# A reordered prologue, filled scan ends and six early output blocks in a hybrid decoder kernel

## Chip, cores and metric

The kernel runs on one core of a Trainium2 chip. The metric is the device time of one execution in microseconds (us). The engines are called PE (matrix products; PEld is its weight load), DVE (vector), ACT (scalar functions), POOL (general) and SP (which here only issues DMA transfers). An fp32 product is two PE instructions, one with the suffix "fp32r" types is one.

## What is computed

The program is a two-layer decoder trunk over T = 272 tokens (16 learned ones and 256 given) of width 2048. The change touches the first layer's mixing part only; what it has to compute, cut from the reference:

```python
h = rms_norm(h0, mix_norm_g)
xx = token_shift(h) - h
xr, xw, xk, xv, xa, xg = (h + xx * mu[i] for i in range(6))
r, k, v = xr @ w_r, xk @ w_k, xv @ w_v
w = -softplus(-(dec_w0 + tanh(xw @ dec_w1) @ dec_w2)) - 0.5
decay = exp(-exp(w))
a = sigmoid(a_w0 + (xa @ a_w1) @ a_w2)
g = sigmoid(xg @ g_w1) @ g_w2
kk = k * k_k, per head of 64 divided by its norm
k = k * (1 + (a - 1) * k_a)
for t in tokens, per head:
    state = state * d_t - (state @ kk_t) (kk_t a_t)^T + v_t k_t^T
    y_t = state @ r_t
out = ((group_norm(y) + bonus) * g) @ w_o
h1 = h0 + out
```

A SwiGLU, a stick-breaking attention and a second SwiGLU follow, from about 730 us on, and are the same in both kernels.

## The kernel before

Everything is kept transposed, channels on partitions and the 272 tokens along the free axis. A 2048x2048 matrix is 16 blocks of 128 output channels; a block is 16 steps k of 128 input channels. In most places a weight w and an activation x are each split in a high and a low part (`whi`, `wlo`, `hi`, `lo`: ACT casts, DVE subtracts), and `mm3k` (L186 to L188) makes one step of three products, whi·hi, whi·lo and wlo·hi; a block then has 48 products of 272 columns.

**Prologue** (L412, `prologue`). `load_tokens` (L313) issues 16 loads of 128x272, in turns on SP's and ACT's queue, with the small vectors on ACT's. ACT squares each (L424), DVE adds four at a time (L428), and PE sums over channels with four fp32 products (L429). ACT takes Ln and Exp (L434, L435), DVE one Newton step. Then the blocks of the key projection w_k: the first G0 = 3 are made with unsplit fp32 weights and activations (L481), k by k in step with the shifted, mixed input x; the other 13 use split weights. `key_out` copies a key block, squares it and adds its squares with an fp32 product into a sum per head, and after the 8th and the 16th block the key norms follow (maximum, Ln, Exp, Newton) and are stored to a scratch in DRAM. Beside them a generator (`rest`) makes the mixed inputs and the three narrow projections (`lr`, dec_w1, a_w1, g_w1; L551), whose weights come in four sets through the pool `wx` (L545), which the split key weights use too.

**Scan** (L617, `scan`). 16 pairs of heads, four chunks of 64 tokens each. Turn n works on four pairs: A = n is finished (states, y, group norm, gate), M = n+1 has its triangular inverse made, B = n+2 is scored, C = n+3 gets decay, iclr and gate from the narrow projections. M's inverse goes through POOL (16x16 blocks, by way of DRAM) and is then widened on PE: `left` (yb) and `right` (zb) for blocks of 16 and 32; yb is followed by a copy on DVE, Ys, which zb reads. A's norm is `parts` (sums per head on PE), an Ln and an Exp on ACT and the last products on DVE. PE and SP take the instructions in the order in which the program writes them; the other engines' order is set by the scheduler at build time.

Between these steps `fill(k)` pulls k steps of three products from `stream`: v and r of all pairs, then 60 steps of the output projection w_o for 4 blocks (15 of their 16 steps; the last needs the last pair). A usual turn takes 32 steps. In the last three turns the number is 0.625 of that. After the scan `wo_first` ends the four blocks, makes the other twelve and adds h0.

The lines that matter: L424 to L442 squares and rstd, L465 to L485 weights and the fp32 blocks, L488 `key_out`, L536 to L553 the narrow projections, L391 to L396 two constants `blk`, L637 to L700 the turns, L772 `stream`, L820 `wo_first`.

Of the kernel before, what the change touches and what calls it, by code (L numbers as in the profile page):

```python
# [25 lines left out]
HD = 64  # L26
# [14 lines left out]
G0 = 3  # L41
# [5 lines left out]
DRAIN = 0.625  # L47
PSTEP = 8
NHEAD = 4
KHEAD = 13  # L50
# [6 lines left out]
def _consts():  # L57
# [14 lines left out]
    put("cen", np.eye(128) - blk / 64)  # L72
    pi = p[:, None] % 64
# [26 lines left out]
    put("blk", blk)  # L100
# [18 lines left out]
class Builder:  # L119
# [99 lines left out]
    def proj(self, src, acts, nk=NK, m=128, late=False):  # L219
        w = self.weights(src, nk, m)  # L220
        out = (self.scbank("mm") if late else self.mmbank())[:m, :acts[0][-1].shape[1]]
# [136 lines left out]
    def time_mix(self):  # L358
# [9 lines left out]
            tc.tile_pool(name="dr", bufs=2, space=bass.MemoryType.DRAM))  # L368
        self.prologue(hid)
        self.o = []  # L370
        self.oraw = []
        with ExitStack() as ctx:
            sp = ctx.enter_context(tc.tile_pool(name="sp", bufs=1, reuse_waits="tile"))
            self.l2 = ctx.enter_context(tc.tile_pool(name="l2", bufs=2, reuse_waits="tile"))
# [32 lines left out]
    def prologue(self, hid):  # L407
# [3 lines left out]
        with ExitStack() as ctx:  # L411
# [33 lines left out]
            def xtile():  # L445
                return pt.tile([128, T], F32, name="xi", tag="xi", bufs=NXL)
# [43 lines left out]
            def key_out(m, ps):  # L490
# [10 lines left out]
                if m % 8 < 7:  # L501
                    return
# [928 lines left out]
```

## Time and profile before

| | us |
|---|---|
| median of 3 runs | 2698.18 |
| lowest and highest of them | 2696.77, 2700.59 |
| the profiled execution | 2704.42 |
| its span | 2702.6 |
| start of the first key product | 28.35 |
| start of the scan's first product (zw) | 174.98 |
| end of the scan's last product wait (L186) | 656.43 |

Rows of a timeline give the start of an instruction or of a run of like ones, its length, engine, line, operation, output<-input, shapes, the number of instructions in the run, and in brackets how long its engine had been idle just before and which instruction it waited for. Rows of the stage table give a window, its length, the busy time of PE, PEld, DVE, ACT and POOL with their instructions, the granted clock of PE (1.00 is 2.4 GHz), the share of the DMA engines and the GB/s moved.

### The profile page before, as it was taken

The numbers are of one execution on the slowest core, as the hardware profiler recorded it, in microseconds if no ns is written. First come the engines' busy times: TensorE is split into PE (matmuls) and PEld (weight loads), VectorE is DVE, ScalarE is ACT, GpSimd is POOL, SyncE is SP. The second block draws the span as 40 slices with busy tenths as digits, with TensorE's granted clock in tenths as the row PEclk, the third lists the DMA queues.
The fourth block names the chain that finished last, engine by engine and source line by source line (L and its number), as shares of the span: only waits on it lengthen the run. The fifth ranks groups of instructions, "written<-read, shape, count | busy, mean of one in ns | idle before, by whom it ended". The sixth has DMA issues, their size and how long they took to land.

```text
span 2702.6 us, 53996 instructions
## 1 busy us (share of the span) xinstructions
PE 2647.7 (98%) x20942; PEld 2452.3 (91%) x20942; DVE 1788.1 (66%) x3610; ACT 1493.0 (55%) x3012; POOL 166.5 (6%) x477
## 2 busy tenths in 40 slices
PE   6999999999999999999999999999999999999999
PEld 5888888888999999999999999988888888888888
DVE  6676767676665555555566875688766666666665
ACT  5675666665544444444445764577555455554553
POOL 0004342431000000000000000000000000000000
PEclk9999999999999999999999999999999999999999
DMA  5434333435555555555655555433665665665655
GB/s 185 140 112 124 101 118 94 125 84 164 172 179 163 188 174 165 187 175 164 187 177 162 183 170 173 158 123 109 194 189 180 195 190 177 201 188 177 198 178 180
DMA packets 185908, 439.50 MB, mean 163 GB/s; under 512 B 58515, under 2 KB 89779, under 8 KB 185651
## 3 DMA queue, kind: packets, MB, share of 16 engines
q1 hardware_dynamic: 183632, 433.23, 51.6%
q8 instruction: 164, 2.69, 0.4%
q10 hardware_dynamic: 2016, 2.82, 0.3%
q14 instruction: 96, 0.76, 0.1%
HBM read 430.24 MB, written 5.74 MB: 161 GB/s over the span
## 4 chain that ended last, share of the span: by engine, by line
PE 92%; DVE 3%; DMA 2%; issue 2%; ACT 2%; POOL 0%; SPq 0%; ACTq 0%; DVEq 0%; POOLq 0%
PE mm L192 22%; PE mm L186 16%; PE mm L188 16%; PE mm L187 16%; PE mm L191 12%; DMA raw<-w_k 1%; PE lr L551 1%; PE mm L481 1%; PE cb L1343 1%; DVE wlo L216 1%; PE cb L1335 1%; PE wa L1292 1%; PE z L972 1%; PE zb L1281 1%; PE yb L1262 1%
## 5 line engine op out<-in xcount | busy, mean ns | idle before, releaser
L168 DVE TENSOR_TENSOR wlo<-raw,whi 128x512 fp32r<-128x512 f32 (+1 forms) x1444 | 977.2, 679 | 613.7 <-ACT whi L167 593.4
L167 ACT CAST whi<-raw 128x512 fp32r<-128x512 f32 (+1 forms) x1444 | 877.6, 610 | 859.6 <-PE mm L187 536.3
L186 PE MATMUL mm<-hl,whi 128*128 128x272 f32 x3344 | 971.1, 291 | 1.5 <-ACT hl L258 1.5
L188 PE MATMUL mm<-hl,wlo 128*128 128x272 f32 x3344 | 966.6, 289 | 0.0
L187 PE MATMUL mm<-hl,whi 128*128 128x272 f32 x3344 | 964.9, 289 | 0.0
L192 PE MATMUL mm<-hl,whi 128*128 128x512 f32 x2624 | 919.8, 394 | 0.0
L191 PE MATMUL mm<-hl,wlo 128*128 128x256 f32 x2624 | 738.2, 282 | 0.0
L186 PEld LDWEIGHTS mm<-hl,whi 128*128 128x128 f32 x3344 | 630.1, 188 | 12.0 <-issue 9.5
L187 PEld LDWEIGHTS mm<-hl,whi 128*128 128x128 f32 x3344 | 636.3, 190 | 0.5 <-issue 0.4
L188 PEld LDWEIGHTS mm<-hl,wlo 128*128 128x128 f32 x3344 | 631.0, 189 | 1.1 <-issue 0.9
L192 PEld LDWEIGHTS mm<-hl,whi 128*128 128x128 f32 x2624 | 492.4, 188 | 112.0
L191 PEld LDWEIGHTS mm<-hl,wlo 128*128 128x128 f32 x2624 | 494.3, 188 | 0.3
L216 DVE TENSOR_TENSOR wlo<-raw,whi 128x512 fp32r<-128x512 f32 (+1 forms) x147 | 101.2, 701 | 36.9 <-ACT whi L215 32.9
L215 ACT CAST whi<-raw 128x512 fp32r<-128x512 f32 (+1 forms) x147 | 88.4, 607 | 61.6 <-PE mm L187 55.0
L208 DVE TENSOR_TENSOR h<-h,mm 128x256 f32<-128x256 f32 (+1 forms) x224 | 93.9, 421 | 6.6 <-PE mm L192 6.0
L186 PE MATMUL mm<-hi,whi 128*128 128x272 f32 x256 | 79.2, 309 | 2.0 <-ACT whi L215 2.0
L201 ACT COPY c<-mm 128x256 f32<-128x256 f32 x104 | 38.8, 373 | 76.7 <-PE mm L192 76.6
L1197 POOL TENSOR_TENSOR Tm<-Ts,As 40x14 f32<-40x14 f32 (+6 forms) x224 | 77.6, 346 | 17.6
L1199 POOL TENSOR_TENSOR Ts<-Ts,Tm 40x14 f32<-40x14 f32 (+6 forms) x224 | 74.7, 333 | 17.6
L188 PE MATMUL mm<-hi,wlo 128*128 128x272 f32 x256 | 74.6, 291 | 0.8 <-DVE wlo L216 0.8
L187 PE MATMUL mm<-lo,whi 128*128 128x272 f32 x256 | 74.3, 290 | 0.0
L186 PEld LDWEIGHTS mm<-hi,whi 128*128 128x128 f32 x256 | 48.8, 191 | 6.6 <-issue 2.4
(285 smaller groups left out, 2317.2 us busy)
## 6 DMA issues: line engine op xcount, KB each, us to landing
raw<-w_gate SPq DMA_DIRECT2D x176, 512.0 KB
raw<-w_up SPq DMA_DIRECT2D x176, 512.0 KB
raw<-w_down SPq DMA_DIRECT2D x128, 512.0 KB
raw<-w_down SPq DMA_DIRECT2D x128, 192.0 KB
raw<-w_v SPq DMA_DIRECT2D x32, 512.0 KB
raw<-w_r SPq DMA_DIRECT2D x32, 512.0 KB
raw<-sb_w_k SPq DMA_DIRECT2D x32, 512.0 KB
raw<-sb_w_v SPq DMA_DIRECT2D x32, 512.0 KB
```

The source lines that it names most:

```text
L167: nc.scalar.copy(hi, part)
L168: nc.vector.tensor_tensor(lo, part, hi.bitcast(F32), ALU.subtract)
L186: mm(out, w[0], x[0], start=first, stop=False)
L187: mm(out, w[0], x[1], start=False, stop=False)
L188: mm(out, w[1], x[0], start=False, stop=last)
L191: mm(out[:, :n], w[1], x[0], start=first, stop=False, skip_group_check=True)
L192: mm(out, w[0], x[2], start=False, stop=last, skip_group_check=True)
L208: self.nc.vector.tensor_tensor(h, h, out[:, c:c + n], ALU.add)
L215: nc.scalar.copy(hi, part)
L216: nc.vector.tensor_tensor(lo, part, hi.bitcast(F32), ALU.subtract)
L1197: V.tensor_tensor(t, Ts[:, 0:i, i:i + 1].to_broadcast([40, i, n]), As[:, i:i + 1, i + 1:].to_broadcast([40, i, n]), ALU.mult)
L1199: V.tensor_tensor(Ts[:, 0:i, i + 1:], Ts[:, 0:i, i + 1:], t, ALU.add)
```

## The change

- **Start.** The tokens come in eight loads of 128x544, all on SP; ACT issues only the vectors. ACT squares two blocks at once, DVE adds the halves, and there are eight fp32 products for the sum in place of four. Eight fp32 products of 128 columns stand ahead of them and eight of 272 columns behind them, whose output nothing reads (`warm`).
- **Key blocks.** Four unsplit fp32 blocks in place of three, so twelve split ones. The narrow projections' weights come in eight sets of two steps through tiles of their own (`l2`), two of the sets ahead of the split key weights on SP's queue. The constants are loaded by SP ahead of these. `key_out` puts each block's sum of squares one block later.
- **Key norms.** The second half's sum and maximum go into turn -3 of the scan and its Ln, Exp, Newton and store into turn -1.
- **`blk`** is cast from the constants that are loaded anyway; its own transfer goes.
- **Fills.** Turn -1, the last before a pair is finished, takes 38 steps in place of 32, of them 2 and then 12 ahead of `left(16)` where 4 and 4 stood; `solve` of the first pair stands one fill of 4 steps behind `norm`'s place in turn -2. The last three turns take other shares (DRAIN of 0.625, 0.63 and 1.2), two of them with single steps behind `chunk0`, `step(2)` and `scores`, and `fill(100)` drains what is left.
- **w_o.** 90 steps in the stream (15 of 16 for six blocks) in place of 60, and a seventh block, 15 steps, in `wo_first` ahead of the first product that needs the last pair.

```diff
-G0 = 3
+G0 = 4
 NWX = 10
 NSQ = 3
 RSTEP = 4
 NXL = 7
 LEAD = 4
-DRAIN = 0.625
+DRAIN = {13: 0.625, 14: 0.63, 15: 1.2}
 PSTEP = 8
 NHEAD = 4
+NTAIL = 2
+NWARM = 8
...
+        nc.scalar.dma_start(self.vecs, self.a["vecs"])
         self.hn = [self.xs2.tile([128, T + 1], F32, name="hn", tag="s") for _ in range(NK)]
-        self.xx = [self.xs2.tile([128, T], F32, name="xx", tag="s") for _ in range(NK)]
-        for k in range(NK):
-            (nc.sync, nc.scalar)[k % 2].dma_start(self.xx[k], self.a["xT"][:, k, :])
-        nc.scalar.dma_start(self.vecs, self.a["vecs"])
+        self.x2 = [self.xs1.tile([128, 2 * T], F32, name="xx", tag="hl") for _ in range(NK // 2)]
+        self.xx = [self.x2[k // 2][:, k % 2 * T:k % 2 * T + T] for k in range(NK)]
+        for k in range(NK // 2):
+            nc.sync.dma_start(self.x2[k].rearrange("p (k t) -> p k t", k=2),
+                              self.a["xT"][:, 2 * k:2 * k + 2, :])
...
-            o, n = CONST["blk"]
-            self.blk = [sp.tile([128, n], F32R, name="blk", tag=f"blk{i}") for i in range(2)]
-            raw = sp.tile([128, n], F32, name="blkf", tag="L")
-            nc.scalar.dma_start(raw, a["consts"][:, o:o + n])
-            nc.scalar.copy(self.blk[0], raw)
-            nc.scalar.activation(self.blk[1], raw, AF.Copy, scale=1.0 / HD)
+            self.blk = [sp.tile([128, 128], F32R, name="blk", tag=f"blk{i}") for i in range(2)]
+            for t, n in zip(self.blk, ("blk", "blk64")):
+                nc.scalar.copy(t, self.cst(n))
...
-            for g in range(0, NK, 4):
-                for k in range(g, g + 4):
-                    sq = pt.tile([128, T], F32, name="sq", tag="sq", bufs=NSQ)
-                    A.activation(sq, xx[k], AF.Square)
-                    if k == g:
-                        acc = sq
-                    else:
-                        V.tensor_tensor(acc, acc, sq, ALU.add)
-                nc.tensor.matmul(ss[:, :T], od, acc, start=g == 0, stop=g == NK - 4)
...
+            warm = self.psd.tile([128, 512], F32, name="warm", tag="sd")
+            for _ in range(NWARM):
+                nc.tensor.matmul(warm[:, :128], od, od, start=True, stop=True)
+            for k in range(0, NK, 2):
+                sq = x0.tile([128, 2 * T], F32, name="sq", tag="hl")
+                A.activation(sq, self.x2[k // 2], AF.Square)
+                s2 = xtile()
+                V.tensor_tensor(s2, sq[:, :T], sq[:, T:], ALU.add)
+                nc.tensor.matmul(ss[:, :T], od, s2, start=k == 0, stop=k == NK - 2)
+            for _ in range(NWARM):
+                nc.tensor.matmul(warm[:, :T], od, s2, start=True, stop=True)
...
+            nc.sync.dma_start(self.consts, a["consts"][:, :NC1])
...
+                s2 = xtile() if m < NK - 1 else self.rstd_p.tile([128, T], F32, name="s2",
+                                                                 tag="rstdt")
                 A.activation(s2, kt, AF.Square, scale=self.vec("k_k", m))
+                late.append((m, s2))
+                if len(late) > 1 and m != NK // 2:
+                    head_sq(*late.pop(0))
+                if m == NK // 2 - 1:
+                    head_sq(*late.pop(0))
+                    key_norm(0, key_max(0))
+                if m == NK - 1:
+                    self.late_keys = late.pop, head_sq, key_max, key_norm
...
-                    if k % 4 == 0:
+                    if k % 2 == 0:
                         w = {}
-                        for i, n in names:
-                            for j, name in enumerate(n):
-                                c = 96 if i < 5 else 128
-                                w[i, j] = wx.tile([128, 4 * c], F32, name="raw", tag="w")
-                                src = a[name] if i < 5 else a[name][j]
-                                nc.sync.dma_start(w[i, j], src[:, k * c:(k + 4) * c])
+                        da = self.l2.tile([128, 512], F32, name="raw", tag="w2", bufs=2)
+                        gg = self.l2.tile([128, 512], F32, name="raw",
+                                          tag="w2h" if k % 4 else "w2l", bufs=1)
+                        for (i, j), t, o, c, src in (
+                                ((1, 0), da, 0, 96, a["dec_w1"]), ((4, 0), da, 192, 96, a["a_w1"]),
+                                ((5, 0), gg, 0, 128, a["g_w1"][0]),
+                                ((5, 1), gg, 256, 128, a["g_w1"][1])):
+                            w[i, j] = t[:, o:o + 2 * c]
+                            nc.sync.dma_start(w[i, j], src[:, k * c:(k + 2) * c])
...
-            f = fill if C else lambda k: fill(k * DRAIN)
+            f = fill if C else lambda k: fill(k * DRAIN[n])
+            if n == NK - 1:
+                self.rot = self.rot[-1:]
...
-                f(4)
+                f(4 if n == -2 else 2)
             if B:
                 B.chunk0()
+            if n >= NK - 2:
+                f(1)
...
-                B.solve()
+                if A or M:
+                    B.solve()
...
-            f(4 if B and not A else 8 + (LEAD if n == -3 else 0))
+            f(12 if M and not A else 4 if B and not A else 8 + (LEAD if n == -3 else 0))
...
+            if n == -3:
+                pop, head_sq, key_max, key_norm = self.late_keys
+                head_sq(*pop())
+                late = key_max(1)
+            elif n == -1:
+                key_norm(1, late)
             f(4)
+            if B and not M:
+                B.solve()
             if M:
                 M.right(16)
...
+                        + [(a["w_o"][m][:, :(KHEAD + 2) * 128], KHEAD + 2)
+                           for m in range(NHEAD, NHEAD + NTAIL)]
...
+        steps += [(m, k) for m in range(NHEAD, NHEAD + NTAIL) for k in range(KHEAD + 2)]
...
+        nh = NHEAD + NTAIL
+        w4 = self.weights(a["w_o"][nh], NK, 128)
+        self.wo.append(self.psd.tile([128, 512], F32, name="mm", tag="sd")[:, :T])
+        for k in range(NK - 1):
+            self.mm3k(self.wo[nh], w4[k], self.o[k], k == 0, False)
```

The scheduler gives ACT this order at the start, before (sq the squares, rstd the inverse root mean square, whi a cast weight):

```order
L424 ACTIVATE sq<-xx 128x272 x3
L485 DMA consts<-consts 128x1198
L424 ACTIVATE sq<-xx 128x272 x13
L434 ACTIVATE rstd<-ss,dv 128x272
L167 CAST whi<-raw 128x512
L435 ACTIVATE rstd<-rstd 128x272
L167 CAST whi<-raw 128x512
L442 ACTIVATE u<-hn,vecs 128x272 x3
```

and with the change:

```order
L319 DMA vecs<-vecs 128x290
L420 ACT_TABLE_LOAD
L434 ACTIVATE sq<-xx 128x544 x8
L444 ACTIVATE rstd<-ss,dv 128x272
L445 ACTIVATE rstd<-rstd 128x272
L452 ACTIVATE u<-hn,vecs 128x272 x3
```

The cast between Ln and Exp is gone, and the consts load is no longer ACT's.

SP's queue behind the token loads, before:

```order
L470 DMA raw<-w_k 128x512 x6
L156 DMA raw<-w_k 128x1024 x14
L545 DMA raw<-dec_w 128x384
L545 DMA raw<-a_w 128x384
L545 DMA raw<-g_w 128x512 x2
L156 DMA raw<-w_k 128x1024 x2
```

and with the change (a second set like the first stands at the three points):

```order
L478 DMA consts<-consts 128x1454
L570 DMA raw<-dec_w 128x192
L570 DMA raw<-a_w 128x192
L570 DMA raw<-g_w 128x256 x2
...
L159 DMA raw<-w_k 128x1024 x17
L533 DMA rkd<-rk 16x272
L159 DMA raw<-w_k 128x1024 x2
```

Two sets of narrow weights have moved ahead of the split key weights, and 17 of these now stand in a row where there were 14.

DVE in the middle of a usual turn of the scan, between the end of A's norm and M's second Ys, before:

```order
L1361 TENSOR_TENSOR sq<-rs_4106 128x272
L1258 STREAM_TRANSPOSE Tn<-Tt 128x256
L1362 SCALAR_TENSOR_TENSOR sq<-vb,sq 128x272
L216 TENSOR_TENSOR wlo<-raw,whi 128x512
L1363 SCALAR_TENSOR_TENSOR rs_4106<-sq,rs_4106 128x272
L1364 TENSOR_TENSOR y<-y,rs_4106 128x272
L216 TENSOR_TENSOR wlo<-raw,whi 128x512
L1365 SCALAR_TENSOR_TENSOR y<-y,dv,bv 128x272
L1267 TENSOR_TENSOR Ys<-yb,consts 128x256
```

and with the change:

```order
L219 TENSOR_TENSOR wlo<-raw,whi 128x512
L1414 TENSOR_TENSOR sq<-rs_4098 128x272
L1311 STREAM_TRANSPOSE Tn<-Tt 128x256
L1415 SCALAR_TENSOR_TENSOR sq<-vb,sq 128x272
L219 TENSOR_TENSOR wlo<-raw,whi 128x512
L1416 SCALAR_TENSOR_TENSOR rs_4098<-sq,rs_4098 128x272
L1320 TENSOR_TENSOR Ys<-yb,consts 128x256
L1417 TENSOR_TENSOR y<-y,rs_4098 128x272
```

Ys has moved ahead of the two products that make y and ahead of one of the two subtractions wlo.

## Rows read from the trace of the kernel before

**Rows 1.** The page, part 1: busy us (share of the span) and instructions.

```profile
PE 2647.7 (98%) x20942; PEld 2452.3 (91%) x20942; DVE 1788.1 (66%) x3610; ACT 1493.0 (55%) x3012; POOL 166.5 (6%) x477
```

**Rows 2.** Timeline of PE, ACT, DVE, 18 to 52 us: start, length, instruction [wait].

```profile
18.85 1.28 PE L429 MATMUL ss<-sq,od 128*128 128x272 f32 x2 [1.54 <-DVE sq L428]
20.16 0.49 ACT L434 ACTIVATE rstd<-ss,dv 128x272 f32<-128x272 f32 x1 [2.07 <-PE ss L429]
23.39 0.62 ACT L167 CAST whi<-raw 128x512 fp32r<-128x512 f32 x1 [2.74 <-DMA raw<-w_k]
23.92 0.42 ACT L435 ACTIVATE rstd<-rstd 128x272 f32<-128x272 f32 x1
28.35 23.94 PE L481 MATMUL mm<-xi,raw 128*128 128x272 f32 x96 [8.22 <-DVE xi L443]
```

**Rows 3.** First rows by line: count, ns of shortest/median/longest, stretch.

```profile
L481 PE MATMUL mm<-xi,raw x13: 392/661/823, 28.3 to 32.9; 128*128 128x272 f32 x13
L429 PE MATMUL ss<-sq,od x8: 657/740/822, 11.2 to 19.5; 128*128 128x272 f32 x8
```

**Rows 4.** Stage table, first 8 us: window, busy by engine, clock, DMA share, GB/s.

```profile
0.00:4.00 4.00, 0.00 (x0) 0.00 (x0) 0.49 (x8) 1.28 (x1) 0.20 (x4) 1.00 0.53 163
4.00:8.00 4.00, 0.00 (x0) 0.00 (x0) 0.76 (x23) 0.00 (x0) 0.00 (x0) 1.00 0.98 325
```

**Rows 5.** Timeline of PE, 51 to 175 us.

```profile
51.93 0.49 PE L186 MATMUL mm<-hl,whi 128*128 128x272 f32 x1
...
171.22 0.29 PE L186 MATMUL mm<-hl,whi 128*128 128x272 f32 x1
...
174.60 0.29 PE L186 MATMUL mm<-hl,whi 128*128 128x272 f32 x1
174.98 0.29 PE L186 MATMUL zw<-dec_w1h,w2h 96*128 96x272 f32 x1
```

**Rows 6.** Stage table, 100 to 140 us.

```profile
100.00:120.00 20.00, 17.86 (x107) 14.50 (x106) 9.33 (x20) 10.52 (x23) 0.00 (x0) 1.00 0.48 151
120.00:140.00 20.00, 18.77 (x102) 15.04 (x102) 12.54 (x27) 12.61 (x29) 0.00 (x0) 1.00 0.34 106
```

**Rows 7.** Timeline of SP's queue, 110 us.

```profile
110.52 0.81 SPq L545 DMA_DIRECT2D raw<-g_w  x2
```

**Rows 8.** Timeline of ACT and PE, 184 to 197 us.

```profile
184.79 0.30 ACT L395 CAST blk<-blkf 128x128 fp32r<-128x128 f32 x1 [3.68 <-DMA blkf<-consts]
...
188.99 0.60 PE L188 MATMUL mm<-hi,wlo 128*128 128x272 f32 x1 [0.79 <-DVE wlo L216]
...
196.38 0.30 PE L1124 MATMUL z<-AR,B 64*64 64x32 f32 x4
```

**Rows 9.** Timeline of POOL and PE, 207 to 227 us.

```profile
207.63 0.74 POOL L1192 TENSOR_TENSOR Ts<-As,consts 40x256 f32<-40x256 f32 x1 [31.37 <-issue]
...
226.06 0.81 PE L1262 MATMUL yb<-Tt,An 64*64 64x64 f32 x13 [0.47 <-DMA Tt<-s]
```

**Rows 10.** Stage row of one scan turn; PE's waits over three turns.

```profile
289.98:317.37 27.39, 26.44 (x361) 23.62 (x361) 19.23 (x50) 17.08 (x41) 10.33 (x29) 1.00 0.38 106
...
PE zb L1281 <- DVE Ys L1267: 2.1, 3, 0.8
```

**Rows 11.** Timeline of DVE and PE, 340 to 346 us.

```profile
340.57 0.44 DVE L1361 TENSOR_TENSOR sq<-rs 128x272 f32<-128x272 f32 x1 [1.18 <-ACT rs L1360]
...
344.28 0.41 DVE L1267 TENSOR_TENSOR Ys<-yb,consts 128x256 f32<-128x256 f32 x1
344.75 0.68 PE L1281 MATMUL zb<-Ys,Tn 64*64 64x64 f32 x16 [0.65 <-DVE Ys L1267]
```

**Rows 12.** Timeline of PE, 645 to 657 us, and its stage row.

```profile
645.82 0.33 PE L1343 MATMUL cb<-Rh,S 64*64 64x64 f32 x4 [0.41 <-ACT S L1345]
...
656.43 0.77 PE L186 MATMUL mm<-hl,whi 128*128 128x272 f32 x4 [1.52 <-ACT hl L258]
...
645.00:650.00 5.00, 4.58 (x31) 4.38 (x32) 1.14 (x2) 3.05 (x6) 0.00 (x0) 0.66 0.17 61
```

More of the change, by code (lines that the diff above doesn't have):

```diff
@@ L72, in _consts @@
     put("cen", np.eye(128) - blk / 64)
+    put("blk", blk)
+    put("blk64", blk / 64)
     pi = p[:, None] % 64
@@ L99, in _consts @@
     first = pos
-    put("blk", blk)
     put("onesD", np.full((128, 128), 1.0 / D))
@@ L220, in proj @@
         w = self.weights(src, nk, m)
-        out = (self.scbank("mm") if late else self.mmbank())[:m, :acts[0][-1].shape[1]]
+        out = (self.psd.tile([128, 512], F32, name="mm", tag="sd") if late else self.mmbank())[:m, :acts[0][-1].shape[1]]
         for k in range(nk):
@@ L368, in time_mix @@
             tc.tile_pool(name="dr", bufs=2, space=bass.MemoryType.DRAM))
+        self.l2 = self.hid_ctx.enter_context(
+            tc.tile_pool(name="l2", bufs=2, reuse_waits="tile"))
         self.prologue(hid)
@@ L440, in mixed @@
             def mixed(i, k, out):
[L441 removed]
+                u = pt.tile([128, T], F32, name="u", tag="u", bufs=NSQ)
                 A.mul(u, hn[k][:, :T], self.vec(f"mu{i}", k))
                 V.scalar_tensor_tensor(out, hn[k][:, 1:], self.vec(f"om{i}", k), u, ALU.mult, ALU.add)
[L445 to L446 removed]
             def mix(i, k, pool):
@@ L700, in scan @@
             f(4)
+        fill(100)
     def load_low(self, A, C):
@@ L789, in stream @@
         self.wo = []
-        for m in range(NHEAD):
-            pool, tag = (self.pmm, "mm") if m < 2 else (self.pfr, "fr")
-            self.wo.append(pool.tile([128, 512], F32, name="mm", tag=tag)[:, :T])
         steps = [(m, k) for m in range(NHEAD) for k in range(KHEAD)]
+        steps += [(m, k) for m in range(NHEAD, NHEAD + NTAIL) for k in range(KHEAD + 2)]
         for m, k in steps + [(m, KHEAD + k) for m in range(NHEAD) for k in range(2)]:
+            if len(self.wo) <= m:
+                pool, tag = ((self.pmm, "mm"), (self.pfr, "fr"), (self.psc, "sc"))[m // 2]
+                self.wo.append(pool.tile([128, 512], F32, name="mm", tag=tag)[:, :T])
             while len(self.o) <= k:
@@ L823, in wo_first @@
         acts = []
-        last = [a["w_o"][m][:, (NK - 1) * 128:] for m in range(NHEAD)]
-        raw = self.wraw.tile([128, NHEAD * 128], F32, name="raw", tag="raw")
-        for m in range(NHEAD):
-            nc.sync.dma_start(raw[:, m * 128:m * 128 + 128], last[m])
-        w = self.whl_pair(raw)
-        for m in range(NHEAD):
-            c = slice(m * 128, m * 128 + 128)
-            self.mm3k(self.wo[m], (w[0][:, c], w[1][:, c]), self.o[NK - 1], False, True)
+        nh = NHEAD + NTAIL
[3 more added lines that the diff above has]
+            self.mm3k(self.wo[nh], w4[k], self.o[k], k == 0, False)
+        for m0, m1 in ((0, NHEAD), (NHEAD, nh)):
+            raw = self.wraw.tile([128, (m1 - m0) * 128], F32, name="raw", tag="raw")
+            for m in range(m0, m1):
+                nc.sync.dma_start(raw[:, (m - m0) * 128:(m - m0) * 128 + 128],
+                                  a["w_o"][m][:, (NK - 1) * 128:])
+            w = self.whl_pair(raw)
+            for m in range(m0, m1):
+                c = slice((m - m0) * 128, (m - m0) * 128 + 128)
+                self.mm3k(self.wo[m], (w[0][:, c], w[1][:, c]), self.o[NK - 1], False, True)
+        self.mm3k(self.wo[nh], w4[NK - 1], self.o[NK - 1], False, True)
         for m in range(NK):
-            ps = self.wo[m] if m < NHEAD else self.proj(a["w_o"][m], self.o, late=m < 2 * NHEAD)
+            ps = self.wo[m] if m <= nh else self.proj(a["w_o"][m], self.o, late=m == nh + 1)
             h = self.hp.tile([128, T], F32, name="h", tag="h")
```

26 lines of the change are left out of this document (15 added, 11 removed).

## The prediction

> **What bounds the kernel now.** I read the page first. PE is busy for 2647.7 us, 98% of the span [rows 1], so time can only be won where PE idles, runs at the low clock or does work that goes away. Both kernels have the same products from the SwiGLU on. The timeline of PE shows where the rest lies: the start, the first turns of the scan, one wait in each turn, and the scan's end.
>
> At the start nothing but the sum of squares is on PE until the first key product at 28.35 [rows 2]. The reader should see the chain ahead of it: last sum 18.85, Ln 20.16, then a weight cast on ACT at 23.39 that had waited 2.74 us for a DMA, and only behind it Exp at 23.92. The first 13 key rows then have a median of 661 ns and fill 4.6 us (28.3 to 32.9) [rows 3]. The granted clock reads 1.00 in these first stages, also where PE has no work [rows 4], so there the column doesn't settle which of the two levels held; durations near twice the later ones I read as the low level. A usual turn takes 27.39 us with PE busy 26.44 [rows 10]. Over three turns zb waits 2.1 us for Ys, up to 0.8 at a time [rows 10]; it is 0.65 in the turn of rows 11. Near the scan's end the granted clock is 0.66 for 5 us, and 1.52 us are lost at 656 [rows 12].
>
> **A, the start: -7.1.** The tokens are 2.23 MB (2048 x 272 x 4 bytes), the vectors 0.15 MB. The DMA engines moved 0.65 MB in the first 4 us and 325 GB/s from then on [rows 4]; 1.73 MB at that rate are 5.3 us, so all is in at 9.3. One more square (0.66, estimated from 0.62 for 512 columns in rows 2), one addition (0.44 as in rows 11) and one slow product (0.66 in rows 3) give the sum at 11.1; before it ended at 18.85 + 1.28 = 20.13 [rows 2]. Ln is 0.49, and from Exp to the first key product it was 4.43 (28.35 less 23.92) [rows 2]. DVE ran two weight subtractions in that stretch, which are gone; I put one of them on the path, 0.7, near the 0.62 of a cast of the same tile [rows 2]. So 0.49 + 4.43 - 0.7 = 4.2, and the first key product starts at 15.4.
>
> The eight idle products behind the sum, 16 rows at 0.23, are 3.7 us and end at 14.8, beside the norm; they cost nothing and I assume the rows behind them then run at the fast level. From 32.9 to 51.93 the other 83 rows took 19.0 us, 0.23 each [rows 3, 5]. Four blocks are 128 rows, 29.4 us: the first split product comes at 44.8, not 51.93. That the fourth block costs 7.4 us (32 rows) is inside this.
>
> The Trainium skill ("TensorE: Matmul & The Clock Gate", Part 1) says that the array starts slow, that activity lets it run fast, that the number of slow products changes from run to run, and that this ramp is under 1% of a typical span. By it the idle products would be worth little in all; here the slow rows cost 4.6 us for 13 where 3.0 would do, 1.6 us, so the trace agrees on the size. Without that gain the sum would be 1.6 us less.
>
> The tokens go from two issuing queues to one. The Trainium skill ("DMA: Bandwidth & Descriptors", "Issuing engines are not separate DMA queues") says that several issuers only save issuing time. By that the change costs nothing, and rows 4 agree so far as the engines were 98% busy from 4 us on; eight issues on SP take no longer than its eight did.
>
> **B, the rest of the prologue: -8.6.** One block fewer of 48 split products: 27 of them lie between 171.22 and 174.60, 3.38 us [rows 5], 0.125 each, so -6.0. From 100 to 140 PE idles 2.14 + 1.23 = 3.4 us [rows 6]. In that stretch the split weights stand behind g_w loads in SP's queue [rows 7], which wait for buffers that the key weights hold. These sets now have tiles of their own and 17 key loads stand ahead of the third. I leave 0.8 of 3.4, so -2.6; bounds 0 and -3.4. The 128 key rows take all of the four large raw buffers, and the next block's load can start only when k = 7 is through, half way at about 30; that is 15 us ahead of its use, no wait. The scan then starts at 174.98 - 15.7 = 159.3.
>
> **C, from zw to the first scores: -4.5.** It takes 196.38 - 174.98 = 21.4 us [rows 5, 8]. In it ACT waits 3.68 for the blk transfer [rows 8], which is now gone; the last key norms, with their table loads, move behind; PE waits on whi and wlo (0.79 at 188.99) [rows 8], and the product there takes 0.60 where it is 0.29 in rows 5. I add up 16.8 us of work without these waits, 4.6 below; I take 4.5, bounds 2 and 6.
>
> **D, to the first yb: -2.3.** From 196.38 to 226.06 it is 29.7 us [rows 8, 9], tied by scores, DMA, some 13 us of POOL from 207.63, DMA [rows 9]. The chain stays. But 6 more steps are pulled beside it, 18 x 0.125 = 2.3 us that later turns need not do. Bounds 0 and -4.
>
> **E, the turns: -7.8.** DVE makes Ys behind two products and two subtractions less than before. Counted back, Exp ends at 340.53 and sq starts at 340.57 [rows 11]; in the new order sq, Tn, the next product, one wlo and rs are some 2.4 us, so Ys starts near 343.0, not 344.28, and zb, at PE's pace due at 344.1, doesn't wait. ACT gets a weight cast of 0.62 [rows 2] between the norm's Ln and Exp, while two copies leave that place, so Exp is about where it was. 12 turns x 0.65 = -7.8. Bounds: 0, and -11 if the rest of the idle 0.95 of a turn [rows 10] goes as well.
>
> **F, the end: -4.6.** Three waits of 0.41 on S [rows 12] now have a step in front: -1.2, and -0.4 in the turn before. The 5 us at 0.66 cost 1.7 over the fast level; I take -1.5 back. The wait of 1.52 at 656 [rows 12] gets the seventh block, 45 products or 5.6 us that must be done anyway: -1.5. Bounds -2 and -7.
>
> Sum: -7.1 - 8.6 - 4.5 - 2.3 - 7.8 - 4.6 = **-34.9**. The profiled execution took 2704.42 us, 1.8 over its span, so this predicts 2669.5 for such a one. The median is 6.2 lower, and I set the sum against it: **2663**.
>
> **The rivals.**
> - *The wait in the turns stays.* Exp comes later because the cast before it or a copy waits for PE, and Ys with it. For: ACT decides when Ys may start, and the new order leaves about 1.1 us (343.0 against 344.1). Against: the stream runs six steps ahead, which frees the cast's buffer six products behind vb. Time 2663 + 7.8 = 2671. Chance 0.18.
> - *PE stays slow through the sums and the idle products.* 16 rows at 0.46 then end at 18.5, the first key product comes 3.6 later, 2667. For: the eight sums of before were all slow, 657 to 822 ns [rows 3]. Chance 0.1.
> - *The moved work does not help.* If chains through POOL and DMA and not PE set the scan's start and its end, C, D and F give nothing: 2663 + 11.4 = 2674. For: POOL's chain is not touched. Against: the rows with waits on ACT and DVE. Chance 0.12.
> - *Slower.* The cast between Ln and Exp is in each turn held until the products behind kv free its buffer, at about 343.1, not 338. Exp ends then near 344, and zb waits 4.2 instead of 0.65: 12 x 3.55 = +43 beside -27 from the rest, **2714**. It decides from 2.25 us a turn more (27/12), a wait of 2.9. Against: with six buffers the one needed is free near 337.4. Chance 0.03.
> - *The idle products and early loads disturb.* Less than the whole of A and B; in the range already.
>
> **How the numbers follow.** The forecast has 0.55, the rivals 0.18, 0.1, 0.12 and 0.03; 0.02 is left for mixtures near no change. The range reaches up to the first and third rival together, 2682, so 2683, and down by the outer bounds of C, D, E and F with some of the idle 0.8 (-1.5, -1.7, -3.2, -2.4, together about -9, and 4 for a run like the lowest): 2650. About 0.2%, 5.4 us, is what a measurement can tell from no change; all cases but the last are beyond that. Faster 0.94, same 0.03, slower 0.03.
>
> **What would show it.** Step by step in the changed kernel: first key product at 15.4 with rows near 0.23, first split product at 45, the scan's first product at 159, the first z 17 us behind it, the first yb at 206, a turn of 26.8 without a wait of zb, no idle of 1 us at the end. The sum is wrong if the turn still takes 27.4, if 0.4 rows appear behind the idle products, or if a wait on raw weights takes the place of those at 100 to 140.

## The result and the profile after

| | before | changed |
|---|---|---|
| median of 6 runs, us | 2701.40 | 2674.89 |
| lowest to highest | 2696.77 to 2702.77 | 2671.90 to 2678.93 |
| profiled execution, its span | 2704.42, 2702.6 | 2674.82, 2673.0 |

The changed kernel is faster by a little under 1%: ratio 0.9908, interval 0.9895 to 0.9921. The medians differ by 26.5 us, the two profiled executions by 29.6. The forecast was 35 less, 2663, in a range from 2650 to 2683.

The page of the changed kernel, part 1, answers to [rows 1]: PE is as busy as before, and the span is shorter by what it idled.

```profile
PE 2648.2 (99%) x20966; PEld 2454.5 (92%) x20966; DVE 1787.8 (67%) x3603; ACT 1485.6 (56%) x3001; POOL 168.1 (6%) x477
```

Where the time went is best read from marks on PE's timeline: starts of the same product in both kernels. "First z" is the scan's first z; the turns' z follow it.

| mark | before | changed | gain so far | of the stretch | forecast |
|---|---|---|---|---|---|
| first split product | 51.93 | 45.30 | 6.6 | 6.6 (A) | 7.1 |
| scan's first product zw | 174.98 | 158.07 | 16.9 | 10.3 (B) | 8.6 |
| first z | 196.38 | 174.84 | 21.5 | 4.6 (C) | 4.5 |
| third z (turn 0) | 243.86 | 225.06 | 18.8 | -2.7 (D) | 0, and 2.3 to come |
| last z (turn 13) | 600.77 | 571.11 | 29.7 | 10.9 (E) | 7.8 |
| ms, the end of w_o | 732.27 | 701.41 | 30.9 | 1.2 (F, and the 2.3) | 4.6 + 2.3 |
| span's end | 2702.6 | 2673.0 | 29.6 | -1.3 | 0 |

The timeline of PE, first 46 us of the changed kernel, answers to [rows 2, 3, 5]:

```profile
1.17 3.75 PE L431 MATMUL warm<-od 128*128 128x128 f32 x16 [1.17 <-DVE od L422]
5.63 2.02 PE L437 MATMUL ss<-xi,od 128*128 128x272 f32 x6 [0.71 <-DVE xi L436]
8.15 3.67 PE L437 MATMUL ss<-xi,od 128*128 128x272 f32 x10 [0.50 <-DVE xi L436]
11.66 3.83 PE L439 MATMUL warm<-xi,od 128*128 128x272 f32 x16
16.06 29.60 PE L489 MATMUL mm<-xi,raw 128*128 128x272 f32 x128 [0.57 <-DVE xi L453]
...
45.30 0.49 PE L189 MATMUL mm<-hl,whi 128*128 128x272 f32 x1
```

The sum's last product starts in a run that ends at 11.8, the idle products end at 15.5, and 0.57 later the key rows begin. In the trace's list by line (count, shortest/median/longest ns, stretch) their median is 392 ns, where the first 13 rows had 661 [rows 3]:

```profile
L437 PE MATMUL ss<-xi,od x16: 392/445/497, 5.6 to 11.4; 128*128 128x272 f32 x16
L489 PE MATMUL mm<-xi,raw x128: 392/392/497, 16.1 to 45.3; 128*128 128x272 f32 x128
```

The stage table from 100 to 140 us, answering to [rows 6], shows PE without idle time, and a usual turn, answering to [rows 10], is 26.6 us long with 0.3 idle:

```profile
100.00:120.00 20.00, 20.00 (x116) 16.83 (x115) 9.68 (x20) 10.80 (x23) 0.00 (x0) 1.00 0.45 137
120.00:140.00 20.00, 20.00 (x128) 17.17 (x127) 9.89 (x19) 12.46 (x25) 0.00 (x0) 1.00 0.35 113
304.90:331.53 26.63, 26.34 (x367) 23.61 (x364) 19.28 (x49) 16.85 (x40) 10.40 (x29) 1.00 0.41 111
```

In such a turn, answering to [rows 11], DVE takes Ys at once behind rs, 2.19 us after sq, where it was 3.71. Timelines of ACT, DVE and PE in one turn:

```profile
370.02 0.61 ACT L218 CAST whi<-raw 128x512 fp32r<-128x512 f32 x1
371.94 0.43 ACT L1413 ACTIVATE rs<-rs 128x272 f32<-128x272 f32 x1
...
372.41 0.45 DVE L1414 TENSOR_TENSOR sq<-rs 128x272 f32<-128x272 f32 x1 [0.50 <-ACT rs L1413]
...
374.15 0.52 DVE L1416 SCALAR_TENSOR_TENSOR rs<-sq,rs 128x272 f32<-128x272 f32 x1
374.60 0.41 DVE L1320 TENSOR_TENSOR Ys<-yb,consts 128x256 f32<-128x256 f32 x1
...
375.94 0.68 PE L1334 MATMUL zb<-Ys,Tn 64*64 64x64 f32 x16
```

Ys is done at 375.01, zb starts at 375.94 and waits for nothing.

Two stretches went worse than forecast. The first is turn -1. SP's queue, then ACT, DVE and PE there, and the stage row:

```profile
185.24 0.43 SPq L793 DMA_DIRECT2D raw<-w_v  x1
196.71 0.30 SPq L1258 DMA_DIRECT2D s<-Ts  x1
...
203.92 0.29 SPq L1214 DMA_DIRECT2D As<-s  x1
204.26 0.46 SPq L793 DMA_DIRECT2D raw<-w_v  x1
...
209.58 0.62 ACT L218 CAST whi<-raw 128x512 fp32r<-128x512 f32 x1 [6.82 <-DMA raw<-w_v]
...
210.23 0.69 DVE L219 TENSOR_TENSOR wlo<-raw,whi 128x512 fp32r<-128x512 f32 x1 [5.59 <-ACT whi L218]
210.84 0.41 DVE L1335 TENSOR_TENSOR Tt<-Tt,zb 128x256 f32<-128x256 f32 x1
...
211.40 1.01 PE L1315 MATMUL yb<-Tt,An 64*64 64x64 f32 x14 [4.09 <-DVE Tt L1335]
...
200.00:220.00 20.00, 15.91 (x180) 14.53 (x179) 8.73 (x21) 5.53 (x13) 9.17 (x29) 0.83 0.59 175
```

From 185.24 to 204.26 SP issues no weight, since the store of POOL's block Ts (196.71) and the transfers behind it stand ahead in its queue. The 14 steps ahead of `left(16)` use up what had been loaded. ACT waits 6.82 for the next weight, DVE has the subtraction wlo ahead of Tt, and PE waits 4.09 for Tt, though zb had made its product at 205. The granted clock of this stage is 0.83, so part of it ran at 1.2 GHz. In the kernel before, SP's queue was held as long by the same transfers, from 207.98 to 228.15, yet PE waited less there, 1.28 and 0.47 us [rows 9], and the clock fell to 0.84:

```profile
225.30 0.30 PE L1262 MATMUL yb<-Tt,An 64*64 64x64 f32 x2 [1.28 <-DMA Tt<-s]
...
220.00:240.00 20.00, 18.26 (x196) 16.44 (x195) 9.83 (x25) 7.53 (x21) 8.96 (x25) 0.84 0.53 146
```

So the held queue is not new; new are the steps that need weights from it while it is held.

The second is `wo_first`: ACT, DVE and PE, and the stage behind the wait:

```profile
637.56 1.90 ACT L170 CAST whi<-raw 128x512 fp32r<-128x512 f32 x3 [5.76 <-DMA raw<-w_o]
...
640.10 1.13 DVE L889 TENSOR_TENSOR h<-h,mm 128x272 f32<-128x272 f32 x3
...
642.79 1.65 ACT L170 CAST whi<-raw 128x512 fp32r<-128x512 f32 x3
...
643.40 1.47 DVE L889 TENSOR_TENSOR h<-h,mm 128x272 f32<-128x272 f32 x4
...
647.51 0.50 DVE L269 SCALAR_TENSOR_TENSOR hl<-h,vecs,hl 128x272 fp32r<-128x272 f32 x1
647.92 2.49 DVE L171 TENSOR_TENSOR wlo<-raw,whi 128x512 fp32r<-128x512 f32 x4
...
648.67 0.39 PE L191 MATMUL mm<-hl,wlo 128*128 128x272 f32 x1 [3.94 <-DVE wlo L171]
...
650.00:655.00 5.00, 5.00 (x30) 5.00 (x30) 4.10 (x8) 2.70 (x5) 0.00 (x0) 0.67 0.81 247
```

Seven blocks of w_o end together. DVE adds h0, gathers squares and splits the seven results from 640.10 to 647.9, and the next weights' wlo comes behind them, though ACT had cast these weights by 644.4. PE stands 3.94 us, and the granted clock is 0.67 in the five us that follow.

### The profile page after: what moved, and what is told of

The parts are those of the page before. It is cut to its first block, busy times and chain, and to the rows that moved or that the text cites. A ratio compares the mean times of both kernels' runs of the same rounds, so it can differ in the third digit from the quotient of the medians.

```text
span 2673.0 us, 54041 instructions
## 1 busy us (share of the span) xinstructions
PE 2648.2 (99%) x20966; PEld 2454.5 (92%) x20966; DVE 1787.8 (67%) x3603; ACT 1485.6 (56%) x3001; POOL 168.1 (6%) x477
## 4 chain that ended last, share of the span: by engine, by line
PE 96%; DMA 1%; DVE 1%; ACT 1%; POOL 0%; issue 0%; SPq 0%; POOLq 0%; ACTq 0%
PE mm L195 23%; PE mm L189 17%; PE mm L191 16%; PE mm L190 16%; PE mm L194 12%; PE mm L489 1%; PE lr L576 1%; PE cb L1396 1%; PE zb L1334 1%; PE yb L1315 1%; PE wa L1345 1%; PE cb L1388 1%; PE z L1025 0%; PE lt L1038 0%; PE ba L1197 0%; DVE G L1205 0%
## 5 line engine op out<-in xcount | busy, mean ns | idle before, releaser
L171 DVE TENSOR_TENSOR wlo<-raw,whi 128x512 fp32r<-128x512 f32 (+1 forms) x1432 | 967.6, 679 | 609.5 <-ACT whi L170 582.6
L170 ACT CAST whi<-raw 128x512 fp32r<-128x512 f32 (+1 forms) x1432 | 869.3, 610 | 850.1 <-PE mm L190 535.9
L219 DVE TENSOR_TENSOR wlo<-raw,whi 128x512 fp32r<-128x512 f32 (+2 forms) x156 | 108.1, 698 | 36.1 <-ACT whi L218 34.8
L218 ACT CAST whi<-raw 128x512 fp32r<-128x512 f32 (+2 forms) x156 | 93.0, 610 | 58.2 <-PE mm L190 44.4
```

What stands on the lines that cost most here:

```text
L170: nc.scalar.copy(hi, part)
L171: nc.vector.tensor_tensor(lo, part, hi.bitcast(F32), ALU.subtract)
L218: nc.scalar.copy(hi, part)
L219: nc.vector.tensor_tensor(lo, part, hi.bitcast(F32), ALU.subtract)
```

## The experiments

Each was run beside the kernel before; "z to ms" is the stretch from the last z to ms (131.5 before, 130.3 changed), "zw to third z" 68.9 and 67.0. Both vary by 3 to 4 us between kernels that don't differ there (65.3 to 68.5 and 129.8 to 133.7), so a smaller difference in them tells nothing by itself.

| run | ratio, interval | zw | zw to third z | turn | z to ms | ms |
|---|---|---|---|---|---|---|
| changed | 0.9908, 0.9895 to 0.9921 | 158.07 | 67.0 | 26.6 | 130.3 | 701.41 |
| e1 | 0.9973, 0.9964 to 0.9983 | 174.53 | 70.7 | 26.7 | 130.9 | 722.77 |
| e2 | 0.9893, 0.9878 to 0.9908 | 157.67 | 62.0 | 26.6 | 131.7 | 697.30 |
| e3 | 0.9872, 0.9855 to 0.9888 | 158.19 | 68.5 | 26.6 | 125.4 | 698.16 |
| e4 | 0.9905, 0.9890 to 0.9920 | 162.13 | 66.5 | 26.6 | 130.8 | 705.45 |
| e5 | 0.9907, 0.9891 to 0.9924 | 161.05 | 68.3 | 26.6 | 129.8 | 705.10 |
| e6 | 0.9863, 0.9848 to 0.9877 | 157.94 | 62.6 | 26.6 | 126.0 | 692.60 |
| e7 | 0.9903, 0.9888 to 0.9917 | 158.21 | 65.6 | 26.6 | 132.1 | 701.94 |
| e8 | 0.9908, 0.9893 to 0.9923 | 158.71 | 70.0 | 26.6 | 133.2 | 707.91 |
| e9 | 0.9904, 0.9889 to 0.9919 | 162.28 | 65.3 | 26.6 | 130.3 | 703.89 |
| e10 | 0.9912, 0.9898 to 0.9927 | 158.02 | 67.6 | 26.6 | 131.1 | 702.80 |
| e11 | 0.9869, 0.9853 to 0.9886 | 157.89 | 64.8 | 26.6 | 124.5 | 693.20 |
| e12 | 0.9915, 0.9898 to 0.9931 | 157.97 | 67.3 | 26.6 | 133.7 | 705.00 |

**e1, the shift alone.** The kernel before with

```diff
-                f(4)
+                f(4 if n == -2 else 2)
-            f(4 if B and not A else 8 + (LEAD if n == -3 else 0))
+            f(12 if M and not A else 4 if B and not A else 8 + (LEAD if n == -3 else 0))
```

> The kernel before with one part of the change: turn -1 pulls 38 steps (2, 12, then six times 4) in place of 32; nothing else. Theory: the stream's place in a turn, six steps further, is by itself what takes the wait of zb away (the v block ends before vb, so ACT's copies leave the place between Ln and Exp, and DVE makes Ys earlier). Then a turn goes from 27.4 to 26.6, -10 over the twelve turns, and the second yb of turn -1 waits some 4 us for Tt, because a weight of the stream lands late behind the inverse's transfers on SP. In all about 6 less than before. Rival: the shorter turn comes from the other edits (fourth fp32 block, later key norms, own tiles for the narrow weights); then a turn stays at 27.4 and the time within 3 of before.

Measured: a turn of 26.7 and no wait of zb in the usual turns, ms 9.5 earlier; the ratio of 0.9973 is 7.3 us. The second yb of turn -1 waited too:

```profile
232.19 0.62 PE L1262 MATMUL yb<-Tt,An 64*64 64x64 f32 x14 [3.12 <-DVE Tt L1282]
```

So the six steps, and nothing else in the change, take the wait out of every turn; and they bring the wait in turn -1 with them. In the order of e1, as in that of the change, the v block's last product now stands two steps ahead of `left(16)`, so ACT copies it before the norm's Ln, not between Ln and Exp. Exp hardly gains by that: it ends 4.16 us behind the start of `vb`, PE's sum ahead of Ln, where it was 4.25. The gain is in DVE's order, 2.20 us from sq to Ys in place of 3.71; why the scheduler sets it so was not looked into.

**e2, the six steps earlier.**

```diff
-LEAD = 4
+LEAD = 10
-                f(4 if n == -2 else 2)
+                f(4)
-            f(12 if M and not A else 4 if B and not A else 8 + (LEAD if n == -3 else 0))
+            f(4 if B and not A else 8 + (LEAD if n == -3 else 0))
```

> The changed kernel, but the six steps more are pulled in turn -3 (LEAD 10) and turn -1 has its 4 and 4 again. Theory: the wait of 4.1 us ahead of the second yb in turn -1, and the low clock behind it, come from 14 steps ahead of left(16), which use up weights that SP cannot load while its queue is held by the inverse's stores; with 8 there the wait goes, a turn stays at 26.6, and the time is 2 to 5 under the changed kernel. Rival: the chain through POOL sets the second yb anyway, and the wait only changes its place (to the first yb, as in the kernel before, 1.3 + 0.5 with 2 us of low clock); then the time is within 1.5 of the changed kernel.

The timeline of PE in turn -1 of this kernel:

```profile
202.89 0.29 PE L1315 MATMUL yb<-Tt,An 64*64 64x64 f32 x2 [1.90 <-DMA Tt<-s]
...
208.10 0.62 PE L1315 MATMUL yb<-Tt,An 64*64 64x64 f32 x14
```

The first yb waits 1.90 for the inverse's own transfer, the second for nothing. From zw to the third z it takes 62.0 in place of 67.0, ms is 4.1 earlier, with a turn still at 26.6. By these marks the theory holds; of the rival there is the 1.9. The medians' intervals overlap those of the changed kernel, so it is the marks that tell them apart.

**e3, the ends spread.** `finish(m)` is the five lines that end a block:

```diff
-        for m in range(NK):
-            ps = self.wo[m] if m <= nh else self.proj(a["w_o"][m], self.o, late=m == nh + 1)
...
+        for m in range(nh + 1, NK):
+            self.wo.append(self.proj(a["w_o"][m], self.o, late=m == nh + 1))
+            for _ in range(min(2, len(self.wo) - len(acts))):
+                finish(len(acts))
```

> The changed kernel, but the residual additions, squares and splits of the seven early blocks of w_o are not written one after the other: two blocks are finished behind each further block of the projection. Theory: the wait of 3.94 us on wlo at 648.67, and the rows at half speed behind it, come from DVE and ACT ending seven blocks in one go (7.8 us on DVE from 640.1 to 647.9) ahead of the next weights; spread, the wait is under 1 us and the time 4 to 5.5 under the changed kernel. Rival: the weights themselves land late (ACT waited 5.8 us for the raw w_o at 637.56, behind seven loads of xT on SP); then PE waits there 3 us or more as before, and the time is within 1.5.

From the last z to ms 125.4, 4.9 less; the stage from 640 to 660, here and in the changed kernel, shows why:

```profile
640.00:660.00 20.00, 20.00 (x162) 20.00 (x161) 19.11 (x43) 15.03 (x33) 0.00 (x0) 1.00 0.82 277
```

```profile
640.00:660.00 20.00, 16.06 (x116) 15.84 (x115) 17.78 (x40) 13.74 (x30) 0.00 (x0) 0.91 0.75 236
```

PE is busy throughout at 1.00. ACT casts the first new weights of w_o no earlier, at 638.35 and 640.46 against 637.56, the last of them as it lands:

```profile
640.46 0.62 ACT L170 CAST whi<-raw 128x512 fp32r<-128x512 f32 x1 [0.97 <-DMA raw<-w_o]
```

The edit also moves loads of xT behind some of w_o's on SP, but as the weights come no earlier, that is not what helps, and the rival falls.

**e4, no idle products.**

```diff
-NWARM = 8
+NWARM = 0
```

> The changed kernel without the sixteen idle products (NWARM 0); what they made is read by nothing. Theory: they keep PE's clock up; without them the first key rows run at some 0.4 us each as in the kernel before (13 rows, 4.6 us), the first split product comes 1.5 to 4 us later than 45.66, and the time is 1 to 4 more than the changed kernel. Rival: DVE and ACT, which make x and its split parts for the rows, set the pace of the key rows; then the first split product moves by less than 1 us and the time by less than 1.

The first split product came at 48.82, 3.5 later, of which 0.7 stand already at the first key product (16.80); ms 4.0 later. The key rows by length, and the stage table (the column behind the POOL time is the granted clock):

```profile
L489 PE MATMUL mm<-xi,raw x128: 392/392/821, 16.8 to 48.8; 128*128 128x272 f32 x128
...
0.00:20.00 20.00, 10.08 (x23) 5.64 (x24) 11.12 (x53) 10.78 (x20) 0.20 (x4) 0.89 0.92 335
20.00:40.00 20.00, 20.00 (x83) 16.32 (x83) 15.89 (x38) 12.39 (x30) 0.00 (x0) 0.94 0.47 145
```

Rows of up to 821 ns are back and the granted clock is at 0.89 and 0.94, so part of the stretch ran at 1.2 GHz. The theory holds by the marks; the ratio alone cannot tell 4 us here.

**e5, three fp32 blocks.**

```diff
-G0 = 4
+G0 = 3
```

> The changed kernel with three unsplit fp32 key blocks in place of four (G0 = 3). Theory, by the terms of the sum: the fourth fp32 block costs 32 rows x 0.23 = 7.4 and saves 48 products x 0.125 = 6.0, so with three the first split product comes 7.4 earlier (38), the scan's first product 1.4 earlier (156.7), and the time is about 1.4 less, if DVE and ACT keep pace. Rival: with three blocks a step k of the key rows has 1.4 us of products but over 1.3 us of DVE, which also has the first split weights to make; then the rows run slower than 0.23, or split products wait behind them, and the scan's first product is 1 us or more later than 158.07.

```profile
40.15 0.39 PE L189 MATMUL mm<-hl,whi 128*128 128x272 f32 x1 [1.78 <-ACT kt L498]
...
16.00:40.00 24.00, 22.27 (x96) 18.16 (x96) 22.40 (x54) 17.92 (x43) 0.00 (x0) 1.00 0.64 207
40.00:60.00 20.00, 19.69 (x128) 17.03 (x129) 12.58 (x25) 14.16 (x34) 0.00 (x0) 0.91 0.55 185
```

The first split product comes at 40.15, 5.2 earlier, not 7.4, behind 1.78 of waiting and with slow rows behind it (clock 0.91), and zw is 3.0 later, not 1.4 earlier. The rows keep their pace (96 in 22.27 us), but split products wait, as the rival said. The chain of that wait has more links than PE's row names: ACT's copy kt stands behind a weight cast that waited for raw w_k, and SP, which loads w_k, had waited from 26 to 37 us for DVE's subtractions wlo, which free the buffers:

```profile
39.19 0.62 ACT L170 CAST whi<-raw 128x512 fp32r<-128x512 f32 x1 [1.33 <-DMA raw<-w_k]
...
SPq L159 <- DVE wlo L171: 8.7, 2, 7.6
```

DVE is busy for 22.4 of the 24 us from 16 to 40. In this order of loads the fourth fp32 block is worth 3 us, since it gives PE work until the split weights are there, and none of that was in my sum of 7.4 against 6.0.

**e6, both edits of e2 and e3.**

> The changed kernel with both edits that helped: the six steps more in turn -3, and the ends of the early w_o blocks spread over the further blocks. Theory: the two losses are apart, so their gains add: the second yb of turn -1 and wo_first wait no longer, ms comes some 8 earlier than the 701.41 of the changed kernel (about 693), ratio to the kernel before near 0.986. Rival: they pay for the same idle time (a later part of the chain, or DMA, sets the end); then ms is within 2 of the better of the two, 697, ratio 0.987 to 0.989.

ms 692.60 (693 expected), ratio 0.9863, median 2666.46. It is 8.8 earlier, where e2 and e3 alone gave 4.1 and 3.3: the two losses are apart and add. This is the fastest kernel of the study; its interval lies below the whole of the changed kernel's.

**e7, four output blocks.**

```diff
-NTAIL = 2
+NTAIL = 0
-DRAIN = {13: 0.625, 14: 0.63, 15: 1.2}
+DRAIN = {13: 0.625, 14: 0.58, 15: 0.58}
```

with `wo_first` of the kernel before and the memory bank that its later blocks use.

> The changed kernel with w_o as before: 60 steps for four blocks in the stream, wo_first of the kernel before, shares of the last turns 0.625, 0.58 and 0.58. Theory: six early blocks and the seventh bring little in the changed kernel, since what they fill (1.52 on ACT at the end, three waits of 0.41, low clock) they lose at the wait of 3.94 on wlo; without them that wait is gone, the 1.52 is back, and the stretch from the last z to ms is within 2 us of the changed kernel's 130.3. Rival: the longer drain is worth its 4.6 as forecast and the wait would be there anyhow; then that stretch is 134 or more.

The wait on wlo is gone; one of 2.43 on DVE and one of 2.84 for the inverse's transfer stand in its place. The stretch is 132.1, 1.8 more, as expected, and inside the 129.8 to 133.7 of the kernels here whose drain is that of the change. Six blocks and a seventh bring nothing measurable as they stand, and some 6 with the ends spread (125.4, 126.0 and 124.5 in e3, e6 and e11).

**e8, blk loaded.**

```diff
-            for t, n in zip(self.blk, ("blk", "blk64")):
-                nc.scalar.copy(t, self.cst(n))
+            raw = sp.tile([128, n], F32, name="blkf", tag="L")
+            nc.scalar.dma_start(raw, a["consts"][:, o:o + n])
+            nc.scalar.copy(self.blk[0], raw)
+            nc.scalar.activation(self.blk[1], raw, AF.Copy, scale=1.0 / HD)
```

> The changed kernel, but the constants blk are loaded by a transfer of their own on ACT's queue and cast from it, as before; the rest is as in the change. Theory: in the kernel before this transfer, for which ACT waited 3.68 us, was a main part of what the first turns lost; with it the stretch from the scan's first product to the first z goes from 16.8 back to 18.5 to 20.5. Rival: ACT's wait lay beside others (late key norms, weights), so the stretch grows by less than 1 us.

From zw to the first z 18.1, 1.3 more: between the two. ACT's wait for the transfer was 3.07, so less than half of it reached PE in that stretch. The 1.0 more from there to the second z is no sign of it: e12, where blk is as in the change, has 1.1 more there too.

**e9, narrow weights as before.** The four-step sets through `wx`:

```diff
-                    if k % 2 == 0:
+                    if k % 4 == 0:
...
+                                w[i, j] = wx.tile([128, 4 * c], F32, name="raw", tag="w")
+                                nc.sync.dma_start(w[i, j], src[:, k * c:(k + 4) * c])
```

> The changed kernel, but the weights of the narrow projections come as before, in four sets of four steps through the pool that the split key weights use too. Theory: the idle 3.4 us from 100 to 140 in the kernel before came from key weights queued on SP behind these sets, which wait for the shared buffers; with four fp32 blocks, which hold eight of the ten at first, the waits are back: the scan's first product 2 to 5 later than 158.07. Rival: one block of split products fewer is what gave the 10.3 us there, and SP has slack; then the scan's first product is within 1 of 158.07.

zw is 4.2 later, of which 0.6 were there at the first split product. PE's waits from 43 to 162 us:

```profile
PE lr L573 <- DVE xi L453: 2.5, 5, 0.6
```

In the changed kernel there is none. So tiles of their own and the earlier place are worth 3.6. PE's wait shows at the narrow projections' inputs, not at the key weights named in the theory; but ACT, which makes these inputs between its casts, has its waits for raw w_k back. Over that stretch here, in the kernel before (50 to 176) and in the changed kernel (43 to 158):

```profile
ACT whi L170 <- DMA raw<-w_k: 15.1, 7, 4.5
...
ACT whi L167 <- DMA raw<-w_k: 13.6, 6, 4.8
...
ACT whi L170 <- DMA raw<-w_k: 2.4, 1, 2.4
```

**e10, key norms in the prologue**, and none in the turns:

```diff
                 if m == NK - 1:
-                    self.late_keys = late.pop, head_sq, key_max, key_norm
+                    head_sq(*late.pop(0))
+                    key_norm(1, key_max(1))
```

> The changed kernel, but the second half of the key norms stays in the prologue, as before. Theory: the norm's two table loads on ACT and its passes on DVE stood in the first turns' chain (z0 is bound by what ACT and DVE make from zw and za), so the stretch from the scan's first product to the first z grows from 16.8 by 1 to 3. Rival: ACT has room there once the transfer of blk is gone, and the stretch stays within 0.7.

From zw to the first z 18.6, 1.8 more, and 2.5 more to the second z, as expected. But the second yb of turn -1, which waits 4.09 in the changed kernel, then waits for nothing (PE waits 0.35 for Tt later, at `wa`), and at the third z 0.6 of the 4.3 is left. The norms' place moves the loss, it hardly changes the sum.

**e11, the steps shared.** Against e6:

```diff
-LEAD = 10
+LEAD = 6
-            f(4 if B and not A else 8 + (LEAD if n == -3 else 0))
+            f(8 if M and not A else 4 if B and not A else 8 + (LEAD if n == -3 else 0))
```

> The kernel with both edits that helped, but only two of the six steps more in turn -3 (LEAD 6) and four in turn -1, ahead of left(16) (4 and 8). Theory: in e6 PE waits 2.42 and 0.4 at the first yb for the inverse's transfer, so a few steps there are free as long as SP's next weight is not needed; with 12 ahead the first wait falls to about 1, the second yb waits under 1, and ms comes 1 to 2 earlier than 692.6. Rival: any step more there uses up the weights that SP can't load in time; then the second yb waits 2 or more and ms is later than 692.6.

The first yb waits 2.15, the second for nothing; ms 693.20 against 692.60, median 2667.56. Neither was right: 2.2 lost up to the third z and 1.5 less from the last z to ms, no more than such stretches vary by.

**e12, squares at once.**

```diff
-                if len(late) > 1 and m != NK // 2:
+                if m < NK - 1:
                     head_sq(*late.pop(0))
                 if m == NK // 2 - 1:
-                    head_sq(*late.pop(0))
                     key_norm(0, key_max(0))
```

> The changed kernel, but each key block's sum of squares follows its block at once on PE, as before, not one block later (the last one stays in the scan). In the kernel before the idle 3.4 us from 100 to 140 showed as PE's kq waiting for ACT's square (0.6, 1.4, 1.1), ACT having waited 4.84 and 1.49 for raw w_k. Theory: the root is the raw weight, which the new order of loads brings in time; then the sum at once costs no more than the copy and the square behind each block, under 1 us each, and the scan's first product comes 0 to 4 later. Rival: it is the place of kq alone; then PE idles 0.8 or more at each of eleven blocks and the scan's first product is 8 or more later.

zw 157.97, PE without a wait from 43 to 162. The later place of kq is worth nothing in the new order of loads. In the kernel before it had shown the wait without being its cause; PE's waits from 50 to 176 us there, and ACT's row:

```profile
PE kq L499 <- ACT xi L496: 2.6, 3, 1.4
...
117.74 0.62 ACT L167 CAST whi<-raw 128x512 fp32r<-128x512 f32 x1 [4.84 <-DMA raw<-w_k]
```

## Why the prediction was right or wrong

The time was inside the range and the sign was right, for the most part by the mechanisms named, but 35 was too much. Between the profiled executions 29.6 are gone, 5.3 less than the sum. That this is so near is in part luck: B and E brought 4.8 more than forecast, D and F 8.4 less. The other 6.6 of the 11.9 us between 2663 and 2674.89 are not in the terms: I took the 6.2 by which the profiled execution of before lay above its median for a constant, but over six runs it was 3.0, and the changed kernel's profiled execution lay at its median.

- **A (7.1, was 6.6).** Right in its steps: first key product at 16.06, forecast 15.4; rows of 0.23 throughout. The sum of squares ended at 11.8, forecast 11.1, and the norm took 4.2 behind it as forecast, where it was 8.22 [rows 2]; which of the loads, the squares and the cast gave how much had no run of its own. That the idle products give the rows their pace is shown by e4, 4.0 in all at ms; the forecast, from the 13 slow rows, had said 1.6. The second rival fell: the sums took 392 to 497 ns. (By its own terms the forecast start is 15.3, not 15.4, and that rival's delay 3.1, not 3.6.) The Trainium skill ("TensorE: Matmul & The Clock Gate", Part 1), which puts such a ramp under 1% of a typical span, agrees with e4 also: 4 of 2675 us are 0.15%.
- **B (8.6, was 10.3).** Mis-sized by 1.7: no idle was left where I had left 0.8, and PE's busy time between these marks fell by 6.8 (119.61 to 112.77) for the 48 products, not by 6.0; why was not traced. Weights late behind the narrow sets were the cause of the idle time, by the row of ACT at 117.74 and by e9, which brings ACT's waits for them back; PE's row named kq.
- **C (4.5, was 4.6).** Right in sum. By e8 and e10, one execution each, it is 1.3 from blk and 1.8 from the norms; for the other 1.5 there is no run.
- **D (no change to the chain, was 2.7 more; 1 to 4.5 in the kernels with the same turn -1).** This step failed: "The chain stays. But 6 more steps are pulled beside it". I costed steps as PE time only and did not look at what feeds them. SP was held by the inverse's transfers for 19 us, as long as before, the loaded weights ran out under the six steps more, and a wait of 4.09 took the place of 1.75 [rows 9], with slow rows behind it as before. e1 shows it in the kernel before, e2 takes it away.
- **E (7.8, was 10.9).** The mechanism was as forecast: Ys 2.19 us behind sq (forecast 2.4), zb not waiting. (The prediction says two subtractions less ahead of Ys; the order shows one less behind sq, and the 2.4 counts it so.) I had multiplied the 0.65 of one turn; the mean of the twelve waits is 0.72, it counts in 13 turns, and a turn is 0.84 shorter (27.45 to 26.61). The wait of zw on G, 0.22, stayed. The first rival (wait stays) and the slower one fell: the cast between Ln and Exp started at 370.02 without a wait.
- **F (4.6 + 2.3, was 1.2).** This step failed: "The wait of 1.52 at 656 [rows 12] gets the seventh block". That wait and the low clock of the last turns went (1.00 in each ten us from 570 to 640), and the waits on S fell from 2.5 us in six to 0.8 in two. But seven blocks ended at once, and the 3.94 on wlo with slow rows behind it took most of it back; two new waits of yb for the inverse's transfer, 1.1 together, took some more. The 1.2 left is less than this stretch varies by. With the ends spread (e3) the stretch is 6.1 shorter than before: so the forecast's 6.9 was nearly there to be had.
- The third rival (moved work doesn't help where chains through POOL and DMA bind) came nearest for D and F, but its cause holds only in part. In D POOL's block held SP's queue (SP waited 11.0 us for it), and PE then waited for weights behind it in the queue, not for the block. In F no POOL or DMA stood in the way, but DVE's ends of seven blocks.
- The last 1.3: from ms to the end the changed kernel takes 1971.6, before 1970.3. Waits of 0.40 and 1.03 on wlo, at 1508.83 and 1834.66, are new. No run was made for them; in the runs above the stretch takes 1970.4 to 1973.3, so 1.3 is no more than it varies by.

## What to carry over

A step of filler is not PE time alone: it takes a weight that some queue must load and two engines must split, so count the loads that its queue can issue before the wait that it is to fill has ended. Work that ends many outputs at once is a burst for the engines which end them; write the ends between the next blocks. And where a wait recurs each turn, look at the phase of the filler before adding anything: six steps, once, shortened each turn by 0.8.

## What the runs showed beyond the expectation

- The wait named in a row can be two engines from its cause: PE's kq on ACT's square stood for a raw weight that was late (ACT 4.84), and moving kq back (e12) cost nothing once the weights came in time.
- Idle products at the start were worth 4.0 us between one execution with them and one without (e4): 2.8 in the 128 key rows (29.60 against 32.37), 0.7 ahead of them, and the rest up to zw.
- The two losses of the changed kernel each had slow rows behind them: granted clock 0.83 from 200 to 220 and 0.67 from 650 to 655, after waits of 4.09 and 3.94; without the second wait it was 1.00 (e3).
